# A decoder trunk whose order is planned: other planner costs, and three tables that move single operations

## The chip, the cores and the metric

The kernel runs on one core of a Trainium2 chip. The core has a matrix engine (TensorE, PE in the profile; its weight loads are PEld), a vector engine (VectorE, DVE), a scalar engine (ScalarE, ACT), a general engine (GpSimd, POOL) and an engine that issues most of the DMAs (SyncE, SP). Every engine runs its own queue in order; they wait for each other through semaphores. The metric is device time in microseconds (us) of one execution, lower is better. Three runs of the kernel before the change took 999.25, 1002.59 and 1001.85 us: a median of 1001.85 us.

## The reference

Two decoder layers work on 256 tokens of width 1024, all in FP32. Each layer adds to `x`, in this order: half a SwiGLU feed-forward (width 2816), a mixer, another half feed-forward, and a gated per-layer embedding. Every one of these reads an RMS norm of `x` and its result is normed again before it is added. The mixer of layer 0 is an mLSTM with 4 heads (two chunks of 128 tokens, exponential gates, a running state); that of layer 1 is differential attention with 8 head pairs, which reads keys and values that were computed once, after layer 0.

```python
for layer in range(DEPTH):
    g = norm_g[layer]
    h = swiglu(rms_norm(x, g[0]), w_ffn_in[layer, 0], w_ffn_out[layer, 0])
    x = x + 0.5 * rms_norm(h, g[1])
    h = rms_norm(x, g[2])
    # layer 0: mlstm_mixer(h, ...), layer 1: diff_attention(h, k_sh, v_sh, ...)
    x = x + rms_norm(h, g[3])
    h = swiglu(rms_norm(x, g[4]), w_ffn_in[layer, 1], w_ffn_out[layer, 1])
    x = x + 0.5 * rms_norm(h, g[5])
    gate = jax.nn.sigmoid(rms_norm(x, g[6]) @ w_ple_gate[layer])
    e = p[layer].astype(x.dtype) @ w_ple_proj[layer]
    x = x + rms_norm(e * gate, g[7])
    if layer == N_A_LAYERS - 1:
        k_sh, v_sh = shared_kv(x, kv_norm, w_kv)
```

## The kernel before

**The work.** The 256 tokens are two row tiles of 128 (`t` is 0 or 1). A weight comes from memory in pieces of 128 x 2048 FP32 (tag `wraw`, ten buffers), is copied by ScalarE into a rounded part (`whi`, six buffers), and VectorE subtracts this from the original to get the remainder (`wlo`, five buffers). Activations are split in the same way (`xh`/`xl`, and `hh`/`hl` for the hidden layer of a feed-forward). A product is then three fast matmuls, high by high, high by low and low by high (`mm3`, line 569). Blocks of a feed-forward's input matrix go mostly in pairs, in a scheme with seven products instead of eight (`block_pair`, line 780); it needs sums of weight blocks, some of which VectorE makes and some an accumulating DMA that GpSimd issues. `forms` (line 762) makes the matching sums of activations. Attention, gates and the mLSTM's inner products use plain FP32 matmuls, which the profile shows as two instructions each.

**Between the blocks** stands a norm: ScalarE squares and sums two halves (`squares`), GpSimd adds the two sums and takes the power -0.5 (`rnorm`, line 632), VectorE adds the scaled result to `x` (`add_to_x`), TensorE transposes `x` (`transpose4`), and the transposed pieces are scaled and split (`gained`, line 710).

**The mLSTM** (line 1072) computes queries, keys and gates, then the values as a block pair, then for each head an exponential and a product (`head`, line 1157), then the outputs of both row tiles (`outputs`, line 1191) with an output gate (another block pair) and an output projection. **Differential attention** is at line 1282.

**The order.** The body is not issued as it is written. `Notes` records every operation with what it must come after; consecutive plain FP32 matmuls or transposes into the same tile count as one operation, and an operation's number is its place in this list (6290 in all). `cost` (line 215) gives each a duration and a latency. `play` (line 309) then simulates the five engines: TensorE takes the ready operation of lowest rank (its place in the program), with a penalty `PEN` where the kind of matmul changes; SyncE takes its loads by rank; ScalarE, VectorE and GpSimd take the ready operation that is due first. Due times come from `backward` (line 270), which counts back from the end of the schedule played before. Ten rounds are played, the best one's due times are used, and all instructions are issued in the resulting order from one line, 495, so that the profile knows them by tile names. An edge between two operations is stored as `after[earlier] = True` (the later one needs the earlier one's result) or `False` (it only has to start after it).

**The start.** ScalarE issues the load of `x0` (the first 128 columns of the transposed input, with gains) and that of another piece of the transposed input (line 596); eight matmuls on a zeroed tile (line 612) run until the first data is there.

## Time and profile before

| | us |
|---|---|
| median of three runs | 1001.85 |
| the profiled execution | 999.12 |
| its span, first to last instruction | 997.3 |
| TensorE busy | 979.6 |
| VectorE busy | 897.7 |
| ScalarE busy | 714.6 |
| GpSimd busy | 95.1 |

A row of the profile's timeline shows the start, the duration, the engine, line, operation, the tile written and those read, the shapes, how often, and in brackets how long the engine stood idle before it and what ended that. Rows of the stretches give, for each window of time, busy microseconds of each engine with the number of instructions, then the granted share of TensorE's clock, the busy share of the DMA engines, and GB/s. Ends of matmuls are modelled, so starts are the better measure. Where the stages lie in the span: feed-forward 1 of layer 0 to about 200 us, mLSTM to about 298, feed-forward 2 to about 480, embedding and keys to about 530, feed-forward 1 of layer 1 to about 695, differential attention to about 797, feed-forward 2 to about 965, then the last embedding.

### The profile page before, as it was taken

To read this page: it belongs to the slowest core of one execution; us is meant where nothing else is said; L and a number is where in the kernel's file an instruction comes from. 1 tells how busy PE (TensorE), PEld (TensorE's weight loads), DVE (VectorE), ACT (ScalarE), POOL (GpSimd) and SP (SyncE) were. 2 spreads that over 40 slices of the span, in tenths; PEclk is the share of its full clock that TensorE was granted. 3 is DMA by queue.
4 is the path that set the end of the run, shared out by engine and by line. 5 is a ranking of instruction groups with operands and counts; after the bars stand their busy time and mean duration, and the time that the engine had idled before them with its cause. 6 is when DMAs were issued, how large, how long until landed. Compare 5 with 4: busy or idle time off the path is not lost. (4 is left out here: it accounts for less than half of the span.)

```text
span 997.3 us, 12405 instructions
## 1 busy us (share of the span) xinstructions
PE 979.6 (98%) x4594; PEld 799.1 (80%) x4594; DVE 897.7 (90%) x898; ACT 714.6 (72%) x954; POOL 95.1 (10%) x133
## 2 busy tenths in 40 slices
PE   8999999999999999999999999999999999999997
PEld 7878888887777788888878888887888877888886
DVE  6999999789989999998798999898875899999983
ACT  7678667588857776776877867687766778767763
POOL 0000000300231000001120000001102200000010
PEclk9999999999999999999999999999999999999999
DMA  9999956976899999766799999764758899996721
GB/s 344 417 312 342 288 217 240 286 246 197 310 346 303 334 295 291 295 244 223 265 312 323 341 346 348 307 253 153 253 211 256 252 284 348 298 281 242 285 85 43
DMA packets 45861, 274.70 MB, mean 275 GB/s; under 512 B 5480, under 2 KB 5864, under 8 KB 16104
## 3 DMA queue, kind: packets, MB, share of 16 engines
q1 hardware_dynamic: 39752, 231.69, 60.8%
q0 software_dynamic: 5760, 41.95, 20.6%
q8 instruction: 36, 0.59, 0.2%
q10 hardware_dynamic: 288, 0.27, 0.1%
q14 instruction: 25, 0.20, 0.1%
HBM read 263.40 MB, written 10.49 MB: 275 GB/s over the span
## 5 line engine op out<-in xcount | busy, mean ns | idle before, releaser
L495 DVE TENSOR_TENSOR wraw<-wraw,wraw 128x2048 f32<-128x2048 f32 x44 | 100.7, 2288 | 0.2
L495 ACT ACTIVATE whi_0r<-wraw 128x2048 fp32r<-128x2048 f32 (+2 forms) x51 | 82.0, 1610 | 10.6 <-PE accI L495 5.7
L495 ACT ACTIVATE whi_2r<-wraw 128x2048 fp32r<-128x2048 f32 (+1 forms) x49 | 79.4, 1633 | 7.5 <-DMA wraw<-in_ffn_in 3.5
L495 ACT ACTIVATE whi_4r<-wraw 128x2048 fp32r<-128x2048 f32 (+1 forms) x45 | 75.3, 1683 | 11.3 <-PE accI L495 5.2
L495 ACT ACTIVATE whi_3r<-wraw 128x2048 fp32r<-128x2048 f32 (+1 forms) x47 | 77.6, 1657 | 8.0 <-PE accI L495 2.5
L495 ACT ACTIVATE whi_1r<-wraw 128x2048 fp32r<-128x2048 f32 (+2 forms) x50 | 74.4, 1502 | 11.6 <-PE accI L495 9.2
L495 ACT ACTIVATE whi_5r<-wraw 128x2048 fp32r<-128x2048 f32 (+1 forms) x43 | 71.8, 1675 | 11.3 <-DVE wraw L495 4.8
L495 ACT ACTIVATE att<-accI 128x512 f32<-128x512 f32 x84 | 49.7, 593 | 39.9 <-PE accI L495 38.7
L495 POOL DMA_DIRECT2D wraw<-in_ffn_in x36 | 32.0, 890 | 336.3 <-DMA wraw<-in_ffn_in 250.4
L495 POOL TENSOR_SCALAR sm<-sm 128x1 f32<-128x1 f32 x32 | 20.7, 648 | 296.6 <-ACT sg L495 295.2
L495 ACT ACTIVATE sg<-att,sm 128x256 f32<-128x256 f32 x57 | 28.3, 504 | 22.7 <-DVE att L495 21.5
L495 POOL TENSOR_TENSOR sm<-sm,mhalf 128x1 f32<-128x1 f32 (+2 forms) x40 | 33.1, 828 | 105.1 <-DVE sm L495 102.6
L495 ACT ACTIVATE sg<-accO 128x512 bf16<-128x512 f32 (+2 forms) x46 | 20.3, 446 | 23.5 <-PE accO L495 17.5
L495 DVE SCALAR_TENSOR_TENSOR wraw<-wraw,sm,wraw 128x512 f32<-128x512 f32 x32 | 22.7, 750 | 13.0 <-POOL sm L495 13.0
L495 PEld LDWEIGHTS tr<-ident,sg 128*128 128x128 f32 x176 | 23.3, 140 | 13.7 <-DVE hl_2r L495 1.9
L495 PE MATMUL tr<-ident,sg 128*128 128x128 f32 x176 | 34.0, 274 | 0.0
L495 DVE TENSOR_TENSOR att<-accI,att 128x512 f32<-128x512 f32 x42 | 28.5, 686 | 2.6 <-PE accI L495 2.6
L495 ACT ACTIVATE sg<-wraw 128x512 bf16<-128x512 f32 x32 | 20.0, 626 | 13.7 <-DVE wraw L495 9.5
L495 DVE SCALAR_TENSOR_TENSOR sg<-att,sm,sg 128x256 f32<-128x256 f32 x57 | 26.5, 483 | 2.0 <-ACT sg L495 2.0
L495 ACT ACTIVATE att<-accI,sm 128x512 f32<-128x512 f32 (+1 forms) x22 | 14.7, 669 | 17.3 <-PE accI L495 17.3
L495 ACT ACTIVATE hh_1r<-tr 128x256 fp32r<-128x256 f32 x30 | 11.3, 378 | 20.1 <-PE accO L495 12.8
L495 DVE TENSOR_TENSOR att<-att,att 128x512 f32<-128x512 f32 (+1 forms) x35 | 23.5, 672 | 1.0 <-ACT att L495 0.9
(612 smaller groups left out, 3251.8 us busy)
## 6 DMA issues: line engine op xcount, KB each, us to landing
wraw<-in_ffn_in SPq DMA_DIRECT2D x102, 1024.0 KB, 7.7
wraw<-in_ffn_out SPq DMA_DIRECT2D x44, 1024.0 KB, 9.2
wraw<-in_ffn_in POOLq DMA_DIRECT2D x36, 1024.0 KB, 13.4
wraw<-in_mlstm_in SPq DMA_DIRECT2D x14, 1024.0 KB, 6.4
wraw<-in_ple_gate SPq DMA_DIRECT2D x8, 1024.0 KB, 5.0
wraw<-in_w_kv SPq DMA_DIRECT2D x8, 1024.0 KB, 4.8
home<-wraw SPq DMA_DIRECT2D x28, 256.0 KB, 5.3
wraw<-home SPq DMA_DIRECT2D x14, 512.0 KB, 4.6
```

Source lines behind the costliest of these rows:

```text
L495: getattr(getattr(self.nc, eng), name)(*args, **kw)
```

## The change

The operations stay the same but for two. What is new:

- Durations: a plain FP32 matmul on 128 rows now costs at least 222 ns where it was at least 105, one on 64 rows 124; a ScalarE operation with a sum costs 60 ns more; only a change between 64-row matmuls and others costs TensorE time in the plan (150 ns), all other changes of kind 5 ns, and the ordering penalty follows the same rule.
- ScalarE's two loads must keep their program order.
- Ten warm-up matmuls instead of eight.
- After the rounds, three tables are applied and the plan is played once more: `FIRST` adds edges (the second operation may only start after the first has started), `SHIFT` adds nanoseconds to due times, and `MOVE` adds to the rank of one or several operations in a row.

```diff
@@ -26,6 +26,44 @@
 ROUNDS = 10
+FIRST = (
+    (4319, 4321), (4319, 4385), (5365, 5244), (5365, 5188), (2092, 2061), (5251, 5220), (5057, 5062), (5222, 5423),
+    (5201, 5235), (4318, 4325), (1595, 1441), (1505, 1440), (1440, 1455), (1535, 1499), (5140, 5139), (4977, 5020),
+    (4975, 5025), (2063, 2264), (2208, 2044), (1464, 1470), (1480, 1500), (1482, 1476), (1664, 1538), (1538, 1458),
+    (1550, 1536), (1480, 1454), (1544, 1547),
+)
+SHIFT = (
+    (138, -12166828), (147, 7213), (173, 7287), (175, 10522), (205, -28563), (266, -41996), (269, -35620),
+    (295, -84784), (331, -55484), (334, -54491), (337, -88941), (338, -45024), (340, -31781), (341, -161489),
+    (343, -108617), (344, -203509), (346, -52943), (386, -11814), (390, -53670), (393, -34537), (394, -168189),
+    (396, -162608), (1308, -58533), (1309, -97295), (1310, -103560), (1313, -111190), (1314, -170957), (1317, 44789),
...
+    (1349, 37223), (1356, -59146), (1359, 29562), (1386, 10525), (1439, -4376737), (1440, -2725461), (1441, -454410),
+    (1454, -4503563), (1455, -3045380), (1458, -4439452), (1460, -152237), (1461, -270420), (1462, -36478),
+    (1464, -4378085), (1466, -175520), (1467, -318667), (1468, -28162), (1470, -4525640), (1472, -2771036),
+    (1473, -2239202), (1474, -44584), (1476, -9725501), (1478, -6966893), (1479, -8294119), (1480, -3303077),
+    (1482, -7409750), (1499, -5487120), (1500, -3890822), (1501, -13100380), (1503, -1333004), (1505, -1059340),
+    (1508, -1816243), (1536, -7027061), (1538, -3542943), (1540, -3727262), (1542, -3900808), (1544, -2367321),
+    (1547, -3499927), (1548, -6014694), (1549, -5635368), (1550, -5657865), (1978, -5999), (1983, -11331),
+    (2043, -7859), (2072, -3500), (2085, -2500), (4197, 1808), (4216, -3878), (4973, -34218), (4977, -25713),
...
+    (5231, -16772), (5244, -26804), (5251, -15422),
+)
+MOVE = (
+    (140, 1, -9250), (183, 1, -1100), (184, 1, -1800), (186, 1, 200), (211, 1, -3350), (212, 1, -2000), (223, 1, 300),
+    (224, 1, 400), (1392, 3, -900), (1395, 1, -700), (1396, 2, -600), (1398, 1, -400), (1442, 1, -11350),
+    (1443, 1, -11600), (1444, 1, -11550), (1445, 1, -11100), (1446, 1, -8250), (1447, 1, -9500), (1448, 1, -7800),
+    (1456, 1, -10550), (1459, 1, -850), (1465, 1, -800), (1471, 1, -2650), (1475, 1, -500), (1477, 1, -700),
+    (1481, 1, -11400), (1510, 1, -950), (1511, 1, -10900), (1512, 1, -10650), (1513, 1, -10350), (1514, 1, -3950),
+    (1559, 1, -4000), (1564, 1, -4550), (1566, 1, -4400), (1568, 1, -4500), (1871, 1, 200), (1877, 1, 300),
+    (4287, 1, -50), (4294, 1, -50), (4296, 1, -50), (4298, 1, -50), (4300, 1, -50), (4342, 1, 400), (4351, 1, 300),
+    (4420, 5, -250), (4970, 1, -200), (4974, 1, -200), (5030, 1, -450), (5032, 1, -750), (5088, 1, -150),
...
+    (5204, 1, -2800), (5221, 1, -2350), (5226, 1, -3250),
+)
...
+        if o.name == "dma_start" and eng == "scalar":
+            if self.ringed is not None:
+                o.after[self.ringed] = False
+            self.ringed = o
...
-        return ins[0].ap[0][1], ins[0].ap[-1][1]
+        return "h" if ins[0].ap[0][1] == 64 else "f"
...
-                o.dur = max(n * 4 / 2.4 / (2 if ins[0].ap[0][1] == 64 else 1) + 6, 70 if n * 4 < P else 105)
-                if n == 1:
-                    o.dur = 210
+                o.dur = 124 if ins[0].ap[0][1] == 64 else max(n / 0.6 + 6, 222)
...
-            o.dur = 0.83 * m + (100 if sb_in else 72) + (90 if ptr else 0) + (90 if sums else 0)
+            o.dur = 0.83 * m + (100 if sb_in else 72) + (90 if ptr else 0) + (150 if sums else 0)
...
-        return 0 if o.kind == before or {o.kind, before} == {"r", "t"} else PEN
+        return PEN if (o.kind == "h") != (before == "h") else 0
...
-                        end += 10 if {o.kind, before} == {"r", "t"} else 110
+                        end += 150 if "h" in (o.kind, before) else 5
...
-    for i in range(8):
+    for i in range(10):
         nc.tensor.matmul(warm[:, :P], wz, wz, start=True, stop=True)
...
-    plan.play(MARGIN, due[ends.index(min(ends))])
+    due = due[ends.index(min(ends))]
+    plan.play(MARGIN, due)
+    for before, then in FIRST:
+        plan.ops[then].after.setdefault(plan.ops[before], False)
+    for i, ns in SHIFT:
+        due[plan.ops[i]] += ns
+    for i, n, by in MOVE:
+        for o in plan.ops[i:i + n]:
+            o.rank += by
+    plan.play(MARGIN, due)
```

## The prediction

> **What bounds the kernel now.** I read the page's span and engine lines first, then TensorE's waits, then busy time by stretch, and last the timeline around each wait.

> ```profile
> span 997.3 us, 12405 instructions
> PE 979.6 (98%) x4594; PEld 799.1 (80%) x4594; DVE 897.7 (90%) x898; ACT 714.6 (72%) x954; POOL 95.1 (10%) x133
> ```

> TensorE is busy for 979.6 of 997.3 us, and the change takes no matrix work away. An order of the same operations can only win back the 17.7 us in which TensorE stands still, and the little that each restart costs. The profiled execution took 999.12 us, 1.8 us more than its span. The three runs shown are 999.25, 1001.85 and 1002.59 us, so this execution stands at their low end, 2.7 us under their median.

> TensorE's waits (us in total, times, longest):

> ```profile
> PE accI L495 <- DVE wraw L495: 1.5, 1, 1.5
> PE accO L495 <- DVE wraw L495: 1.5, 1, 1.5
> PE accI L495 <- DVE xh_0r L495: 1.5, 1, 1.5
> PE accO L495 <- ACT whi_3r L495: 1.4, 1, 1.4
> PE accI L495 <- ACT att L495: 1.3, 3, 0.7
> PE tr L495 <- DVE wraw L495: 0.4, 2, 0.2
> PE accI L495 <- DVE xl_6r L495: 0.5, 1, 0.5
> ```

> Single waits in many places, none that repeats through the run. Busy time by stretch (us, then PE, PEld, DVE, ACT, POOL busy) says what stands beside them:

> ```profile
> 25.00:175.00 150.00, 148.62 (x671) 121.04 (x670) 147.26 (x120) 108.38 (x107) 6.71 (x12) 1.00 0.88 303
> 215.00:268.00 53.00, 50.40 (x225) 39.74 (x224) 50.14 (x67) 48.41 (x77) 4.80 (x3) 1.00 0.79 259
> 268.00:290.00 22.00, 22.00 (x105) 18.06 (x104) 19.55 (x25) 10.86 (x19) 5.39 (x6) 1.00 0.95 279
> 290.00:350.00 60.00, 57.79 (x258) 46.17 (x258) 58.00 (x49) 45.27 (x51) 8.74 (x9) 1.00 1.01 336
> 690.00:704.00 14.00, 13.28 (x69) 10.67 (x68) 10.94 (x15) 10.13 (x19) 5.82 (x8) 1.00 0.35 105
> 790.00:850.00 60.00, 59.46 (x268) 47.49 (x267) 58.75 (x54) 47.35 (x51) 7.43 (x9) 1.00 0.95 309
> 850.00:950.00 100.00, 100.00 (x455) 81.60 (x453) 98.24 (x81) 71.44 (x74) 1.72 (x2) 1.00 0.79 268
> 950.00:1000.00 50.00, 40.24 (x208) 33.97 (x207) 27.28 (x38) 20.75 (x43) 6.95 (x13) 0.95 0.18 64
> ```

> TensorE's idle time is length less PE: 1.38 us in the first feed-forward block (25 to 175), 2.60 in the mLSTM's values, heads and gates (215 to 268), 2.21 where the second block starts, 0.72 where diff-attention starts, 0.54 where the last block starts. Of the 9.8 us in the last row, 2.7 lie behind the span's end and the rest is the final norm and store, which no table touches. VectorE has 2.74 us idle in 25 to 175 and 1.25 in 790 to 850: there it is a second bound.

> **What a stall costs.** Around 60 us:

> ```profile
> 58.23 0.40 PE L495 MATMUL accI<-wlo_2r,xh_4r 128*128 128x512 f32 x1
> 58.01 1.91 ACT L495 ACTIVATE whi_3r<-wraw 128x2048 fp32r<-128x2048 f32 x1 [0.41 <-ACT att L495]
> 59.98 0.51 PE L495 MATMUL accO<-whi_3r,hh_1r 128*128 128x512 f32 x1 [1.35 <-ACT whi_3r L495]
> 60.33 0.39 PE L495 MATMUL accI<-wlo_3r,xh_6r 128*128 128x512 f32 x1
> 60.56 0.40 PE L495 MATMUL accI<-whi_1r,xl_6r 128*128 128x512 f32 x1
> ```

> Undisturbed matmuls start 0.23 us apart (60.33 to 60.56). Across the stall it is 1.75 and then 0.35, so 1.52 + 0.12 = 1.64 us are lost where 1.35 show as idle: a toll of 0.28 us per stall, which I add below.

> **The change part by part.** Numbers in the tables count the noted operations; I followed each to its instruction in the trace.

> *The two loads on ScalarE's queue* now keep program order, x0 first:

> ```profile
> 0.72 0.41 ACTq L495 DMA_DIRECT2D wraw<-in_xT  x1
> 1.16 0.45 ACTq L495 DMA_DIRECT2D att<-in_x  x1
> 1.04 3.58 PE L495 MATMUL tr<-sg 128*128 128x128 f32 x16 [1.04 <-DVE sg L495]
> 5.64 0.29 DVE L495 TENSOR_SCALAR xh_0r<-att 128x128 fp32r<-128x128 f32 x1 [4.65 <-DMA att<-in_x]
> 6.07 0.47 PE L495 MATMUL accI<-whi_0r,xh_0r 128*128 128x512 f32 x1 [1.45 <-DVE xh_0r L495]
> ```

> x0 ends the first real wait, and is issued 1.16 - 0.72 = 0.44 us sooner. Between 0 (the next loads are no earlier) and 0.44 I take **-0.3**, since TensorE then runs almost without a hole up to 20 us.

> *Two more warm-up matmuls* are four instructions of 3.58/16 = 0.22 us, 0.9 us behind the end at 4.62. The hole up to 6.07 (5.6 with x0 sooner) covers them: **0**. Without that cover they would cost 0.9.

> *First feed-forward block.* The entries from 138 to 396 let the Silu at 19.45 and its transposes run as soon as they can, and make fourteen conversions and adds of weights or sums due 12 to 204 us sooner, so that VectorE takes them whenever they are ready. They aim at 0.21 us idle at 20.5 and 1.35 at 60. Bounds 0 and 1.64; with VectorE at 147.26 of 150 I take half, **-0.8**: what TensorE gains at 60, VectorE must deliver sooner at 75 to 175.

> *mLSTM.* Entries 1308 to 1568 give some eighty operations an order of their own: the heads' exponentials and products, the value copies, the splits between them (due up to 13 ms sooner, so at once when ready) and the matmuls of outputs(0) (rank about 4500 lower, ahead of everything).

> ```profile
> 222.81 0.50 PE L495 MATMUL accI<-whi_2r,xh_3r 128*128 128x512 f32 x1 [0.33 <-ACT att L495]
> 257.63 0.50 PE L495 MATMUL accI<-whi_3r,xh_4r 128*128 128x512 f32 x1 [0.69 <-ACT att L495]
> 265.89 0.47 PE L495 MATMUL accO<-whi_1r,xh_0r 128*128 128x512 f32 x1 [1.45 <-DVE wraw L495]
> ```

> Full gain: 2.60 idle and three tolls, 3.44 us; none: 0. ScalarE is at 48.41 of 53 here but has 11 us free from 268 to 290, so some of its work can wait. What is late next is the weight split 1500, which FIRST now puts behind the last head's exponential, and the block pair's matmuls on it. Two thirds: **-2.3**.

> *Start of the second block* (1978 to 2264):

> ```profile
> 293.19 3.14 POOL L495 TENSOR_SCALAR sm<-sm 128x1 f32<-128x1 f32 x1 [7.43 <-ACT sg L495]
> 293.95 2.29 DVE L495 TENSOR_TENSOR wraw<-wraw,wraw 128x2048 f32<-128x2048 f32 x1
> 297.81 0.66 PE L495 MATMUL accI<-ident,wraw 128*128 128x128 f32 x4 [1.48 <-DVE wraw L495]
> ```

> 1.48 of its 2.21 us hangs on GpSimd's 3.14 us sum, which no entry names. Of the other 0.73 and three tolls (1.6) I take **-0.3**.

> *Start of diff-attention.* FIRST puts 4318 (the split xh_6r) ahead of a square and 4319 (xl_6r) ahead of 4321 (the second att product):

> ```profile
> 693.61 0.61 ACT L495 ACTIVATE sg<-wraw 128x512 bf16<-128x512 f32 x1
> 693.64 0.69 DVE L495 TENSOR_TENSOR att<-accI,gcol 128x512 f32<-128x512 f32 x1
> 694.22 0.61 ACT L495 ACTIVATE xh_6r<-att 128x512 fp32r<-128x512 f32 x1
> 695.42 0.68 DVE L495 TENSOR_TENSOR xl_6r<-att,xh_6r 128x512 fp32r<-128x512 f32 x1
> 696.15 0.50 PE L495 MATMUL accI<-whi_1r,xl_6r 128*128 128x512 f32 x1 [0.47 <-DVE xl_6r L495]
> ```

> xh_6r can start 0.6 us sooner and xl_6r about 1, more than the wait of 0.47: 0.75 with its toll, out of 1.28 for both stalls here. **-0.85**.

> *Start of the last block* (4970 to 5423): 5201, the add that frees an accumulator, goes ahead of the 2.29 us add 5235, which then waits some 3 us, and with it the two splits of its weight. The stretch holds 0.54 us and three tolls, 1.4; VectorE is full up to 950 (98.24 of 100), so **-0.6**, bounds 0 and 1.4.

> *Corrected durations* cost no instruction, but re-sort VectorE, ScalarE and DMAs everywhere, also where no table repairs it. Each conversion that moves also moves the release of its raw buffer, and with it SyncE's next load and everything behind that in the queue. The trace cannot show the new order. From above it is at most the stalls already counted; from below, the second rival. I take **+0.6**.

> Sum: -0.3 - 0.8 - 2.3 - 0.3 - 0.85 - 0.6 + 0.6 = **-4.55 us**. From 999.12 that is 994.6, from the median of 1001.85 it is 997.3. Rows don't say why the runs differ; I take the middle, **996.0**.

> **Rivals.**
> *VectorE takes the gain back.* In 25 to 175 and 790 to 950 it is at 98%, so each stall removed returns as a wait for a split, and the mLSTM's as a wait for the split that was put back. Only x0 and diff-attention stay, about 1.2: 997.9 and 1000.7, the middle 999.3. Against it: ScalarE's free time after 268. It is also where the tables would end if they no longer fit the order they shift.

> *GpSimd is blocked at the layer ends* (the slower side). Its sums and powers behind each norm:

> ```profile
> L495 POOL TENSOR_TENSOR sm<-sm,mhalf x40: 559/568/2455, 18.7 to 992.3; 128x1 f32<-128x1 f32 x32, 128x4 f32<-128x4 f32 x4, 128x2 f32<-128x2 f32 x4
> L495 POOL TENSOR_SCALAR sm<-sm x32: 292/302/3138, 18.3 to 989.0; 128x1 f32<-128x1 f32 x32
> ```

> Minimum, median, maximum in ns: 302 normally, 3138 at 293, ending as the 2.29 us VectorE add beside it ends. A re-sorted VectorE can put such an add beside any norm. Price 1.48 + 0.28 = 1.76 us of TensorE for each that matters; it decides once the matmuls left cover less than the 2.84 us of delay. Three more against a gain of 1.2 make +4.1: 1003.2 and 1005.9, the middle 1004.6. For it: one of these is already on the path. Against: TensorE's only other waits on a norm (tr for wraw, above) come to 0.4 us.
> [...]

> *The start decides the spread.* If the 2.6 us between the median and the lowest run arise in the first microseconds and the longer warm-up removes them, the median falls to 999.25 - 4.55 = 994.7. For it: the hole of 1.45 us after the warm-up. Against: the granted clock shows no start in the page's slices.
> [...]

> *Everything comes off:* 0.44 + 1.64 + 3.44 + 1.6 + 1.28 + 1.4 = 9.8 us, 989.3 and 992.1: 990.7.

> **How the numbers follow.** Forecast 0.53 (its own range 992 to 999), VectorE 0.22, GpSimd 0.13, start 0.08, everything 0.04; 0.3% (3 us) is about what this kernel's measurement can tell. Faster: most of 0.53, and 0.12: 0.60. Same: VectorE's 0.22 and a little of the first: 0.27. Slower: 0.13. Range 991 to 1002: it takes in VectorE's case at either base and leaves out the whole of GpSimd's and part of the last.

> **What would show it.** Right: TensorE idle falls from 2.60 us to under 1 in the mLSTM stretch; no wait for xl_6r near 695; the first real matmul near 5.6; the whi_3r wait near 60 gone or halved. VectorE's rival: the same waits, 10 to 100 us further on, for wlo or whi tiles. GpSimd's: a sum or power of over 2 us just ahead of transposes that wait for wraw. The forecast is wrong if TensorE's idle time stays above 16 us, or drops below 9.

## The result, and the profile after

The changed kernel takes **990.85 us** (median of four runs, 990.61 to 991.39). The kernel before, timed beside it, takes 1001.14 us. The ratio is 0.9899, with a 95% interval of 0.988 to 0.9918: 1.0% faster. I had forecast 996.0 with a range of 991 to 1002. The direction is right; the time lies 0.15 us below the lower end, and the gain is about twice the forecast one.

The two profiled executions took 999.12 us before and 990.61 us after: 8.5 us, which is also the difference of the spans. The medians differ by 10.3 us, since the profiled execution of before was one of its quickest. Over all comparisons below, before had medians of 1000.2 to 1000.44 us, so its usual time is some 9.5 us above the new kernel's.

The page's span and busy time of the engines, after (to be read against the first fence of the prediction):

```profile
span 988.8 us, 12411 instructions
PE 977.0 (99%) x4598; PEld 798.9 (81%) x4598; DVE 896.0 (91%) x898; ACT 714.7 (72%) x954; POOL 99.7 (10%) x133
```

TensorE now stands still for 988.8 - 977.0 = 11.8 us instead of 17.7. That explains 5.9 of the 8.5 us. The other 2.6 us left TensorE's *busy* time, although it has four more instructions. The prediction did not count on anything of the kind beyond the toll of 0.28 us per stall.

TensorE's waits after (us in total, times, longest):

```profile
PE tr L536 <- DVE wraw L536: 1.1, 1, 1.1
PE tr L536 <- DVE sg L536: 1.0, 1, 1.0
PE accI L536 <- ACT att L536: 0.7, 1, 0.7
PE accI L536 <- DVE wlo_1r L536: 0.7, 1, 0.7
PE accI L536 <- ACT whi_1r L536: 0.5, 1, 0.5
PE accI L536 <- DVE wlo_0r L536: 0.2, 1, 0.2
```

Six waits of over 0.15 us are left; the second is the one ahead of the warm-up. The waits for `whi_3r`, `xh_0r` and `xl_6r` are gone. Of the 11.8 us of idle time, 7.1 lie behind the last matmul, after as before; ahead of it 10.6 us have become 4.7.

The same stretches as in the prediction, after (us, then PE, PEld, DVE, ACT, POOL busy, granted clock, DMA share, GB/s):

```profile
25.00:175.00 150.00, 150.00 (x676) 122.01 (x676) 147.82 (x122) 108.92 (x107) 7.50 (x13) 1.00 0.88 307
215.00:268.00 53.00, 51.06 (x229) 39.79 (x228) 50.10 (x65) 46.96 (x77) 4.00 (x4) 1.00 0.76 252
290.00:350.00 60.00, 58.88 (x269) 47.64 (x267) 59.14 (x52) 46.60 (x52) 9.22 (x8) 1.00 0.97 321
690.00:704.00 14.00, 14.00 (x79) 11.20 (x79) 12.66 (x16) 9.17 (x23) 4.70 (x6) 1.00 0.64 228
790.00:850.00 60.00, 60.00 (x269) 48.45 (x269) 59.73 (x54) 46.38 (x52) 7.95 (x6) 1.00 1.00 330
```

The first feed-forward, the start of diff-attention and the start of the last block have no idle time left (1.38, 0.72 and 0.54 before). The mLSTM keeps 53 - 51.06 = 1.94 of its 2.60 us, and the start of the second block 1.12 of 2.21. All of this is idle time. What a stage really gained is seen when both executions are set side by side at points where TensorE has done the same work, and the times are compared. Matmuls are matched by count and size, so these differences are good to some 0.1 us:

| TensorE's work, by its time before | after less before, us | predicted |
|---|---|---|
| up to 22 us (start) | -0.60 | -0.3, and part of -0.8 |
| 57 to 109 (first feed-forward) | -1.30 | rest of -0.8 |
| 200 to 281 (mLSTM) | -0.37 | -2.3 |
| 291 to 303 and 313 to 420 (second block) | -0.84 and -1.2 | -0.3 |
| 420 to 692 | -0.1 | 0 |
| 692 to 704 (start of diff-attention) | -1.03 | -0.85 |
| 704 to 787 (rest of diff-attention) | -1.8 | 0 |
| 818 to 850 (last block) | -1.21 + 0.33 | -0.6 |
| the rest | -0.4 | +0.6, over the whole run |
| sum | -8.5 | -4.55 |

Three rows do not fit: the mLSTM gave a sixth of what I expected, the second block several times as much, and diff-attention behind its start 1.8 us for which I had no term at all.

Two rows of the table, the start's and the mLSTM's, are partly chance of this one execution, as the runs below show. The matmul that starts at 20.48 us before and at 19.87 here starts between 20.38 and 21.15 in e3, e4, e6, e7 and e8, which all load x0 first. And the wait for `whi_1r` at 224 us stands in none of e4, e5, e7 and e8, which have the same mLSTM; there the mLSTM row is -1.2. The two all but cancel in the sum: e4's span is 989.0 us.

### The profile page after: what moved, and what is told of

Read it like the earlier page. It is cut to its first block, busy times and chain, and to the rows that moved or that the text cites. A ratio compares the mean times of both kernels' runs of the same rounds, so it can differ in the third digit from the quotient of the medians.

```text
span 988.8 us, 12411 instructions
## 1 busy us (share of the span) xinstructions
PE 977.0 (99%) x4598; PEld 798.9 (81%) x4598; DVE 896.0 (91%) x898; ACT 714.7 (72%) x954; POOL 99.7 (10%) x133
## 5 line engine op out<-in xcount | busy, mean ns | idle before, releaser
L536 ACT ACTIVATE whi_0r<-wraw 128x2048 fp32r<-128x2048 f32 (+2 forms) x49 | 79.5, 1633 | 12.7 <-DVE wraw L536 4.7
L536 ACT ACTIVATE whi_1r<-wraw 128x2048 fp32r<-128x2048 f32 (+2 forms) x50 | 77.7, 1567 | 8.4 <-DVE wraw L536 4.0
L536 ACT ACTIVATE whi_3r<-wraw 128x2048 fp32r<-128x2048 f32 (+1 forms) x46 | 74.2, 1616 | 10.4 <-PE accI L536 4.4
L536 ACT ACTIVATE whi_5r<-wraw 128x2048 fp32r<-128x2048 f32 (+1 forms) x46 | 77.3, 1688 | 5.9 <-PE accI L536 3.3
L536 POOL TENSOR_SCALAR sm<-sm 128x1 f32<-128x1 f32 x32 | 29.1, 909 | 287.2 <-ACT sg L536 281.7
L536 ACT ACTIVATE sg<-att,sm 128x256 f32<-128x256 f32 x57 | 28.4, 502 | 18.7 <-DVE att L536 17.9
L536 POOL TENSOR_TENSOR sm<-sm,mhalf 128x1 f32<-128x1 f32 (+2 forms) x40 | 28.9, 722 | 101.5 <-DVE sm L536 98.9
L536 DVE TENSOR_TENSOR wlo_0r<-wraw,whi_1r 128x2048 fp32r<-128x2048 f32 (+1 forms) x13 | 25.3, 1955 | 3.8 <-PE accI L536 3.5
L536 ACT ACTIVATE hh_2r<-tr 128x256 fp32r<-128x256 f32 x30 | 11.3, 378 | 21.2 <-PE tr L536 10.1
L536 DVE TENSOR_TENSOR wlo_2r<-wraw,whi_0r 128x2048 fp32r<-128x2048 f32 (+1 forms) x12 | 25.2, 2108 | 1.4 <-ACT whi_0r L536 1.1
```

Of the source, the lines that this page charges most:

```text
L536: getattr(getattr(self.nc, eng), name)(*args, **kw)
```

## The experiments

The 12 kernels below were timed in three groups, each beside runs of the kernel before. Ratios are to these runs, with their 95% interval.

### Costs, tables and start, each alone

*e1: the corrected durations and the new start, with empty tables.*

```diff
-FIRST = (
-    (4319, 4321), (4319, 4385), ...
+FIRST = ()
-SHIFT = (
-    (138, -12166828), (147, 7213), ...
+SHIFT = ()
-MOVE = (
-    (140, 1, -9250), (183, 1, -1100), ...
+MOVE = ()
```

> The changed kernel with the three tables emptied: corrected durations, x0 loaded first and ten warm-up matmuls stay. Theory T (the tables hold the gain): only the start's 0.6 to 0.7 us comes off, the time stays within 2 us of before (about 1000.5), and the 64-row matmuls of diff-attention still stand in five runs. Theory C (the corrected durations hold a good part): the 64-row matmuls fall into four runs, diff-attention gets about 1.7 us shorter, and the time is 998 or lower.

Measured: 997.25 us (996.54 to 1003.85, 12 runs), ratio 0.9981 [0.9968, 0.9994], span 995.3. With the new start the re-sort wins about 3 us of median and 2.0 us of span (the ratio says 1.9, because two of the 12 runs lie above 1001), where I had put +0.6 for it alone. But it makes one stall longer, as e1's timeline shows:

```profile
694.86 0.68 DVE L504 TENSOR_TENSOR xl_6r<-att,xh_6r 128x512 fp32r<-128x512 f32 x1
695.60 0.50 PE L504 MATMUL accI<-whi_1r,xl_6r 128*128 128x512 f32 x1 [1.50 <-DVE xl_6r L504]
```

The wait for `xl_6r` is 1.50 us; before it was 0.47. The whole is faster in spite of it, mostly between 704 and 790 us (-1.6) and 291 and 303 us (-1.26).

*e2: the tables and the new start, on the old durations and the old rule for a change of kind.*

```diff
-        return "h" if ins[0].ap[0][1] == 64 else "f"
+        return ins[0].ap[0][1], ins[0].ap[-1][1]
...
-                o.dur = 124 if ins[0].ap[0][1] == 64 else max(n / 0.6 + 6, 222)
+                o.dur = max(n * 4 / 2.4 / (2 if ins[0].ap[0][1] == 64 else 1) + 6, 70 if n * 4 < P else 105)
+                if n == 1:
+                    o.dur = 210
...
-            o.dur = 0.83 * m + (100 if sb_in else 72) + (90 if ptr else 0) + (150 if sums else 0)
+            o.dur = 0.83 * m + (100 if sb_in else 72) + (90 if ptr else 0) + (90 if sums else 0)
...
-        return PEN if (o.kind == "h") != (before == "h") else 0
+        return 0 if o.kind == before or {o.kind, before} == {"r", "t"} else PEN
...
-                        end += 150 if "h" in (o.kind, before) else 5
+                        end += 10 if {o.kind, before} == {"r", "t"} else 110
```

> The changed kernel with the durations and the penalty for a change of matmul kind put back to those of before; tables, load order and warm-up stay. Theory A (the tables are corrections of single stalls that hold by themselves): most of the gain stays, under 994 us. Theory B (they only fit the order that the corrected durations give): the gain is gone, 999 us or more, with new waits of 1 to 2 us for wlo or whi tiles where entries move operations past each other.

Measured: 1001.35 us (1000.33 to 1003.15, 10 runs), ratio 1.0012 [1.0003, 1.0021], span 998.7. TensorE's longest waits in e2:

```profile
PE accO L538 <- DVE att L538: 2.1, 1, 2.1
PE accI L538 <- ACT whi_3r L538: 1.8, 1, 1.8
PE accI L538 <- ACT att L538: 1.5, 2, 0.7
```

On the other durations, the same entries make new and longer waits in the mLSTM: 2.1 us at 244.3 and 1.8 us for a `whi_3r` at 248.6. Behind the first of them the granted clock drops, and stands at 0.50 from 246 to 252 us:

```profile
245.00:253.00 8.00, 6.20 (x17) 3.95 (x16) 8.00 (x8) 7.38 (x17) 0.00 (x0) 0.57 0.79 285
```

6.20 us of matmuls at a mean clock of 0.57 lose some 2.7 us, an estimate from this row. All ten runs of e2 have a mean clock of 0.994 to 0.996, where e3's have 0.996 to 0.999, so the drop is probably in all of them. With e3 below, these are the four corners, all but the last measured with the same runs of before:

| | without tables | with tables |
|---|---|---|
| old durations, new start | 999.81 (e3) | 1001.35 (e2) |
| new durations, new start | 997.25 (e1) | 990.85 (the change) |

The tables win 6.4 us on the new durations and lose 1.5 us on the old ones. The loss has one place. Set beside e3 by equal work, e2 is 4.4 us longer in the mLSTM (200 to 281 us), the clock included, and 0.9 longer at 303 to 420; it is 2.6 us shorter at 290 to 303, 1.1 at 692 to 704 and 0.7 at 810 to 850. So, by place, the mLSTM's entries are repairs to one particular order and do harm on another. The later ones win on either, though not the same amounts.

*e3: only the new start, on the kernel before.*

```diff
+        if o.name == "dma_start" and eng == "scalar":
+            if self.ringed is not None:
+                o.after[self.ringed] = False
+            self.ringed = o
...
-    for i in range(8):
+    for i in range(10):
```

> The kernel before with only its start changed: x0 loaded first and ten warm-up matmuls. Ledger: the first real matmul comes 0.6 to 0.75 us sooner and all else stays, so -0.6 us, and the runs spread as widely as those of before (3 us). Theory S (the start makes the spread of before): the median falls by 2 us or more, to the lowest runs of before, and the runs agree within 1 us.

Measured: 999.81 us (999.01 to 1001.31, 11 runs), ratio 0.9996 [0.9987, 1.0004], span 997.9. The timeline of its first microseconds:

```profile
4.75 0.50 PE L506 MATMUL accI<-whi_0r,xh_0r 128*128 128x512 f32 x1
...
5.89 0.50 PE L506 MATMUL accI<-wlo_0r,xh_0r 128*128 128x512 f32 x1 [0.40 <-DVE wlo_0r L506]
...
7.35 0.51 PE L506 MATMUL accI<-whi_0r,xh_0r 128*128 128x512 f32 x1 [0.27 <-ACT whi_0r L506]
...
8.08 0.51 PE L506 MATMUL accI<-wlo_0r,xh_0r 128*128 128x512 f32 x1 [0.22 <-DVE wlo_0r L506]
```

The first real matmul starts at 4.75 instead of 6.07, without any wait. But now it waits for the copies and remainders of the first weights, and by 22 us only 0.08 us of the 1.3 is left. The load of x0 ended last, with these close behind.

*e4: the change with eight warm-up matmuls.*

```diff
-    for i in range(10):
+    for i in range(8):
```

> The changed kernel with eight warm-up matmuls instead of ten. Theory S: some runs are 1.5 to 3 us longer than the changed kernel's 990.6 to 991.4, with a lower granted clock at the start. Otherwise: the same time within 0.5 us and the same spread.

Measured: 990.89 us (990.77 to 990.97, 4 runs), ratio 0.9906 [0.9891, 0.992], span 989.0. The two warm-up matmuls make no difference, neither to the median nor to the spread.

### The tables, a part at a time

Each of these takes all entries of one range of operation numbers out of the three tables and leaves the rest of the change.

```diff
 e5: -  (138, -12166828), ... (396, -162608)  in SHIFT, (140, 1, -9250) ... (224, 1, 400) in MOVE
 e6: -  12 pairs of FIRST, 54 entries of SHIFT and 27 of MOVE with numbers from 1000 to 1600
 e7: -  15 pairs of FIRST, 26 entries of SHIFT and 36 of MOVE with numbers above 1600
```

*e5: without the entries of the first feed-forward (numbers below 1000).*

> The changed kernel without the table entries of the first feed-forward block (operations below 1000). If its gain stands on its own: the wait of some 1.4 us for a split weight near 57 to 60 us comes back and the rest of the trace stays, 992 to 992.5 us. If VectorE gives it back further on (the prediction's first rival): within 0.4 us of the changed kernel.

Measured: 993.74 us (992.88 to 996.12, 4 runs), ratio 0.9938 [0.9919, 0.9957], span 991.1. Its profile loses 2.3 us against the changed kernel: about 1 by 21 us and 1.2 between 57 and 107 us. The first of these is not shown to be the entries' work, since e4, e6 and e7, which have them, lose 0.7 to 1.3 us there as well. At the second this wait stands, in a stage where the changed kernel has none:

```profile
59.97 0.51 PE L674 MATMUL accI<-wlo_3r,xh_6r 128*128 128x512 f32 x1 [0.88 <-DVE wlo_3r L674]
```

Of this loss at most 0.3 us comes back by 200 us. So VectorE, 98% busy in this stage, does not take the gain back.

*e6: without the mLSTM's entries (numbers 1000 to 1600, more than half of SHIFT).*

> The changed kernel without the table entries of the mLSTM (operations 1000 to 1600). The prediction's step: they are worth 2.3 us, so 993.2. By the ledger of the two profiled runs, in which the stretch 200 to 280 us gained 0.4 us and the kernel without tables gained the same there: nothing, 990.9 within 0.5 us, with other waits in that stretch but the same sum.

Measured: 990.27 us (990.12 to 990.79, 4 runs), ratio 0.9899 [0.9883, 0.9916], span 989.0. For the whole kernel these entries are worth nothing. The mLSTM's stretch and its largest waits in e6:

```profile
215.00:268.00 53.00, 50.42 (x228) 40.06 (x228) 50.50 (x66) 47.72 (x76) 4.78 (x3) 1.00 0.77 258
```

```profile
256.05 2.00 PE L611 MATMUL accO<-wraw,att 128*128 128x257 f32 x8 [0.76 <-DVE wraw L611]
264.11 0.47 PE L611 MATMUL accO<-whi_3r,xh_0r 128*128 128x512 f32 x1 [0.70 <-DVE wraw L611]
```

And the changed kernel's, with the entries:

```profile
244.52 0.50 PE L536 MATMUL accI<-wlo_1r,xh_1r 128*128 128x512 f32 x1 [0.72 <-DVE wlo_1r L536]
250.86 0.50 PE L536 MATMUL accI<-whi_0r,xh_5r 128*128 128x512 f32 x1 [0.75 <-ACT att L536]
```

2.58 us idle without, 1.94 with, and the same time. The entries remove the waits for the heads' products at 256 and 264 and put waits for a weight's remainder and for a head's `att` at 244.5 and 250.9 in their place. In the comparison by equal work of the changed kernel with the one before, the same is seen: -1.68 us between 259 and 270, where the wait of 1.45 was, and +1.9 between 224 and 247. Of the latter 0.7 hang on a wait that is not the entries' doing. It stands in the changed kernel's profile alone; e4, e7 and e8 run the same matmuls in the same order there (e5 too, with other buffers) and lack it. The wait, and e4's stretch without it:

```profile
224.09 0.50 PE L536 MATMUL accI<-whi_1r,xh_0r 128*128 128x512 f32 x1 [0.46 <-ACT whi_1r L536]
```

```profile
215.00:268.00 53.00, 51.52 (x231) 40.52 (x230) 50.76 (x66) 47.59 (x77) 4.17 (x4) 1.00 0.77 256
```

So with the entries the mLSTM has about 1.5 us of idle time and is 1.2 us shorter than before from 200 to 281 us; in e6, without them, it is 0.4 to 0.5 us shorter. The entries do win some 0.7 us in their own stage, and lose it at the norm behind it. From 291 to 303 us e6 is 0.7 us shorter than the changed kernel and 1.1 shorter than e4: TensorE's wait near 296 is 0.43 us in e6, 1.12 and 1.51 in those two, behind a GpSimd sum that is as long in all three (4.29, 4.21, 4.21).

*e7: without the entries above 1600 (second block, diff-attention, last block).*

> The changed kernel without the table entries from operation 1600 on (second feed-forward block, diff-attention, last block). By the ledger against the kernel without tables: 1.4 us at 300 to 420, 2.3 us at 692 to 704 (the wait for xl_6r comes back), 1.2 us at 818 to 829, so 4.9 us and 995.8. The prediction's steps for the same places say 0.3 + 0.85 + 0.6 = 1.75 us, so 992.6.

Measured: 996.1 us (995.49 to 998.63, 7 runs), ratio 0.9958 [0.9943, 0.9972]. Its profiled execution was its slowest (998.63, span 996.9), so I use its places and not its sum. Against the changed kernel it loses 2.4 us at 288 to 300, 1.4 at 310 to 345, 2.3 at 688 to 698 and 1.2 at 810 to 841, the three starts that the entries name. Most of the first is not the entries' worth but the clock, which drops to a half behind a wait of 2.06 us:

```profile
297.58 0.66 PE L627 MATMUL tr<-ident,wraw 128*128 128x128 f32 x4 [2.06 <-DVE wraw L627]
```

```profile
298.00:302.00 4.00, 4.00 (x17) 3.29 (x15) 3.42 (x7) 3.43 (x9) 1.78 (x3) 0.57 0.90 179
```

4.00 us of matmuls at a mean clock of 0.57 lose 1.7 us, an estimate from this row. The loss at 697 is e1's wait again:

```profile
697.20 0.50 PE L627 MATMUL accI<-whi_3r,xl_6r 128*128 128x512 f32 x1 [1.50 <-DVE xl_6r L627]
```

So what the tables win lies in the entries that e5 and e7 leave out: 2.9 and 5.3 us by medians (together more than the tables' 6.4, so they overlap). The mLSTM's add nothing to the whole.

### GpSimd at the start of the second block

The prediction's slower rival rests on GpSimd's sums being blocked by VectorE's adds. In the changed kernel this happens at the same place as before, and worse. From its timeline:

```profile
290.18 2.28 DVE L536 TENSOR_TENSOR wraw<-wraw,wraw 128x2048 f32<-128x2048 f32 x1
290.55 4.21 POOL L536 TENSOR_SCALAR sm<-sm 128x1 f32<-128x1 f32 x1 [7.14 <-ACT sg L536]
292.38 2.29 DVE L536 TENSOR_TENSOR wlo_3r<-wraw,whi_4r 128x2048 fp32r<-128x2048 f32 x1
295.43 1.41 DVE L536 SCALAR_TENSOR_TENSOR wraw<-wraw,sm,wraw 128x512 f32<-128x512 f32 x2 [0.76 <-POOL sm L536]
296.24 0.66 PE L536 MATMUL tr<-ident,wraw 128*128 128x128 f32 x4 [1.12 <-DVE wraw L536]
```

The sum takes 4.21 us: it starts during one add and ends with the *second*. *e8* puts the second one, and two like it, behind the norm:

```diff
 FIRST = (
+    (1809, 1888), (1809, 1866), (4968, 5048),
```

> The changed kernel with three more pairs in FIRST: VectorE's second add of the norm's result to x (1809) ahead of the splits 1888 and 1866, and 4968 ahead of the add 5048. So VectorE waits for GpSimd instead of starting another operation with two SBUF inputs. If GpSimd is blocked for as long as such operations follow each other: the sum near 290.5 takes under 2.4 us instead of 4.21, the transposes of x lose their wait of 1.12 us near 296, and that place gets 1.4 us shorter. If the sum is slow for another reason it stays above 4 us. The moved splits may cost the same again: 989.5 to 991.5 in all.

Measured: 992.07 us (992.01 to 992.93, 4 runs), ratio 0.992 [0.9905, 0.9934], span 990.3. The place itself, in e8's timeline:

```profile
289.85 2.28 DVE L537 TENSOR_TENSOR wraw<-wraw,wraw 128x2048 f32<-128x2048 f32 x1
290.21 2.08 POOL L537 TENSOR_SCALAR sm<-sm 128x1 f32<-128x1 f32 x1 [7.17 <-ACT sg L537]
...
293.78 0.66 PE L537 MATMUL tr<-ident,wraw 128*128 128x128 f32 x4 [0.62 <-DVE wraw L537]
294.31 2.29 DVE L537 TENSOR_TENSOR wlo_3r<-wraw,whi_4r 128x2048 fp32r<-128x2048 f32 x1
```

The mechanism is confirmed: with one add in the way the sum ends with that one, after 2.08 us, and TensorE's wait falls from 1.12 to 0.62. The whole kernel is still slower than the changed one, by 1.2 us. The repair wins 0.43 us here and loses 0.49 at 310 to 325, 0.65 at 446 and 1.04 at 800, where other tiles (`xl_3r`, `hl_2r`, an `att`) are now late. The loss at 446 may be chance, for e5 has one of 0.5 us there without the pairs. The three pairs were not tried apart.

### The rule for changes of kind

In diff-attention the scores (`accO<-wraw,wraw`) are matmuls on 64 rows, for the two heads of a pair on rows 0 to 63 and 64 to 127 in turn; between their groups stand matmuls on 128 rows. Before, the plan charged 110 ns and an ordering penalty for most changes of kind; the change charges only a change into or out of 64 rows. *e9* puts this rule alone into the kernel before, without new durations, tables or start.

```diff
-        return ins[0].ap[0][1], ins[0].ap[-1][1]
+        return "h" if ins[0].ap[0][1] == 64 else "f"
...
-        return 0 if o.kind == before or {o.kind, before} == {"r", "t"} else PEN
+        return PEN if (o.kind == "h") != (before == "h") else 0
...
-                        end += 10 if {o.kind, before} == {"r", "t"} else 110
+                        end += 150 if "h" in (o.kind, before) else 5
```

> The kernel before with one part of the corrected durations alone: a change of matmul kind costs 150 ns in the plan where 64-row matmuls begin or end and 5 ns elsewhere, and the ordering penalty follows; no other duration, no table. If this rule is what shortens diff-attention: the 64-row matmuls stand in four runs instead of five, and 704 to 790 us gets 1.6 to 1.7 us shorter. If the corrected FP32 durations do it: five runs, and no gain there. The other stretches move by 1 to 2 us either way, so the whole time says little.

Measured: 993.2 us (992.01 to 993.58, 4 runs), ratio 0.9921 [0.9907, 0.9935], span 991.8. Alone, these three lines give 7.2 us by medians, where the whole change gives some 9.5. What they do in diff-attention is seen in the timeline of before, round its last scores:

```profile
729.73 0.40 PE L495 MATMUL accI<-whi_3r,xl_2r 128*128 128x512 f32 x1
730.05 2.05 PE L495 MATMUL accO<-wraw,wraw 64*128 64x128 f32 x24
732.03 0.39 PE L495 MATMUL accO<-hl_1r,hh_1r 128*128 128x256 f32 x1
732.35 1.16 PE L495 MATMUL accO<-wraw,wraw 64*128 64x128 f32 x8
733.44 0.50 PE L495 MATMUL accI<-whi_0r,xh_0r 128*128 128x512 f32 x1
```

and of the changed kernel:

```profile
724.12 0.39 PE L536 MATMUL accI<-whi_0r,xl_2r 128*128 128x512 f32 x1
724.43 2.16 PE L536 MATMUL accO<-wraw,wraw 64*128 64x128 f32 x32
726.52 0.50 PE L536 MATMUL accI<-whi_5r,xh_0r 128*128 128x512 f32 x1
```

Before, one 256-wide matmul splits the 32 instructions into 24 and 8, and from the matmul ahead to the matmul behind it takes 733.44 - 729.73 = 3.71 us; unsplit it takes 2.40. The matmul in between must run somewhere, at an estimated 0.12 us (half of the 0.23 between two undisturbed 512-wide ones); the other 1.2 us are the split. TensorE shows no idle time in either, so no wait tells of it. The scores stand in four groups (16, 32, 16, 32) in e1, e9 and the changed kernel alike, against five before, and from 704 to 790 us these three gain 1.6, 1.5 and 1.8 us. So the split is most of it, and the rest, 0.3 to 0.6 us, was not traced.

The rest of e9's 5.5 us of span comes from elsewhere: -2.19 at 291 to 303, where the wait of 1.48 behind GpSimd is gone, -1.12 at 692 to 704 and -0.76 at 57 to 109. The rule also moves matmuls there (it no longer charges a change between fast and plain 128-row matmuls); which of them matter was not tried.

*e10: e1 with the three pairs of FIRST that name xl_6r's split.*

```diff
-FIRST = ()
+FIRST = ((4319, 4321), (4319, 4385), (4318, 4325))
```

> The kernel without tables, and with three pairs of FIRST alone: 4318 ahead of 4325, 4319 ahead of 4321 and of 4385. Without them TensorE waits 1.5 us for xl_6r near 695 us. If single stalls are worth their idle time and a toll of 0.28 us: that wait goes, the stretch of 690 to 704 us gets 1.5 to 2.3 us shorter and the whole 1.5 to 2.3 us less than the 997.25 of the kernel without tables: 995 to 995.7. If VectorE gives it back, the wait reappears within 20 us and the time stays at 997.

Measured: 997.07 us (996.49 to 997.65, 5 runs), ratio 0.9963 [0.995, 0.9976], span 994.9. The wait for `xl_6r` is gone, and 692 to 704 is 2.40 us shorter than in e1. But the plan behind it comes out otherwise, and in e10 the scores stand in six groups:

```profile
702.72 1.16 PE L505 MATMUL accO<-wraw,wraw 64*128 64x128 f32 x16
...
710.94 1.26 PE L505 MATMUL accO<-wraw,wraw 64*128 64x128 f32 x16
...
712.56 1.26 PE L505 MATMUL accO<-wraw,wraw 64*128 64x128 f32 x16
...
720.37 1.16 PE L505 MATMUL accO<-wraw,wraw 64*128 64x128 f32 x16
...
727.75 2.05 PE L505 MATMUL accO<-wraw,wraw 64*128 64x128 f32 x24
...
730.04 1.16 PE L505 MATMUL accO<-wraw,wraw 64*128 64x128 f32 x8
```

The stages with a split group lose 0.47 and 1.14 us, and with smaller losses elsewhere 0.4 us of span is left of the 2.4. One edge repairs one stall and re-sorts everything behind it.

### Can the plan do better?

*e11 and e12* add more pairs to FIRST, chosen only because the plan's own end falls: in e11 131 pairs on top of e6 (planned end 983.5 to 982.5 us), in e12 two pairs that keep GpSimd free at 290 us and 154 others (982.6).

```diff
 e11: FIRST = (the pairs left in e6) + 131 more
 e12: FIRST = (the pairs left in e6) + ((1809, 1888), (1809, 1866)) + 154 more
```

> The changed kernel without the table entries of the mLSTM, and with 131 more pairs of FIRST that shorten the planner's own schedule by 1.0 us (983.5 to 982.5). If the planner's end still tells the chip's time to some tenths: 989.3. If what is left are waits that the planner doesn't know (GpSimd beside VectorE, loads at the start): 990.3, as without these pairs.

> As the kernel before in this list (no mLSTM entries, more pairs: 154, planner's end 982.6), and VectorE's add 1809 ahead of the splits 1888 and 1866, so that GpSimd's sum behind the mLSTM isn't blocked for two VectorE operations. If that wait (0.4 to 1.1 us near 296) is real and nothing gives it back: 988.7 to 989.5, the fastest of all. If the moved splits cost it again, as they did with the changed kernel: 990 to 990.5.

Measured: e11 992.59 us (991.57 to 993.32, 5 runs), ratio 0.9915 [0.9903, 0.9928]; e12 991.01 us (990.49 to 991.54, 4 runs), ratio 0.9901 [0.9888, 0.9915]. Neither beats e6, from which both start. The plan ends 5.9 us ahead of the measured span in the changed kernel (982.9 and 988.8) and 8.2 us in the kernel before (989.1 and 997.3): a microsecond in the plan is below what it knows of the chip.

No kernel here is clearly faster than the changed one: e6's 990.27 us and e12's 991.01 us cannot be told from its 990.85 us.

## Why the prediction was right and wrong, step by step

- **x0 first, -0.3: too large.** e3 measured -0.08 by 22 us. Its bound of 0 ("the next loads are no earlier") is what happened. The -0.60 of the changed kernel's own execution is luck, as said below the table. The first real matmul, forecast near 5.6, starts at 5.33 in the changed kernel and at 4.75 in e3, with the same start: the 20 warm-up instructions took 4.60 us in the one and 3.91 in the other.
- **Two warm-up matmuls, 0: right** (e4). The hole covers them.
- **First feed-forward, -0.8: mis-sized.** The wait at 60 is gone whole, not halved: -1.30 from 57 to 109, and e5 gives 1.2 there. I took half because VectorE is 98% busy; its 2.74 us of idle time in 25 to 175 were enough (2.18 are left).
- **mLSTM, -2.3: wrong.** It gave -0.37, or -1.2 without the chance wait at 224, and e6 shows that its entries give the whole kernel nothing. The failed step is "two thirds" of a bound that assumed each wait gone without a successor. The old wait at 266 did go (-1.68), but a weight's remainder became late at 244 and an `att` at 251 (0.72 and 0.75), the kind of successor that I had named and priced at a third. The 0.7 us that the entries still win here are lost at the norm behind the mLSTM, which I counted as another stage. My sign for it, under 1 us of idle time in this stretch, failed too: 1.94, and 1.5 in e4.
- **Start of the second block, -0.3: too small.** It gave -0.84 and -1.2, and e7 without its entries loses 3.8 us there, 1.7 of them by the clock. I assumed that a wait behind GpSimd which no entry names would stay. It did: 1.12 for 1.48 here, 1.51 in e4, and GpSimd's sum even took longer, 4.21 for 3.14. The rest of the stage, to 420 us, gained as much again, and there I had no term.
- **Start of diff-attention, -0.85: right.** -1.03. Of the step as written, the wait goes, and xl_6r comes sooner by 0.6 us (3.87 us behind the start of the add to `x`, against 4.47). But xh_6r comes only 0.06 sooner, since ScalarE now waits for its `att`. In the changed kernel's timeline:

```profile
689.62 0.63 ACT L536 ACTIVATE xh_6r<-att 128x512 fp32r<-128x512 f32 x1 [0.45 <-DVE att L536]
690.28 0.69 DVE L536 TENSOR_TENSOR xl_6r<-att,xh_6r 128x512 fp32r<-128x512 f32 x1
```

- **Start of the last block, -0.6: about right**, -0.9.
- **Corrected durations, +0.6: wrong in sign, and the main error.** I bounded their gain "at most the stalls already counted". That is false: they change how long TensorE is *busy*. The rule for changes of kind keeps the groups of 64-row matmuls whole, some 1.2 of the 1.5 to 1.8 us in diff-attention, and no wait shows it. e1 gives about -3 us for all costs and the start, e9 -7.2 us for the rule alone; so the rest of e1 costs some 4 us on top of the rule, and the tables then win 6.4. I read the diff's line on the changes of kind as a planner's detail and did not look for 64-row matmuls in the trace.
- **The tables are tied to their durations.** I treated the entries as additive. The four corners say -6.4 us on one set of durations and +1.5 on the other, where the mLSTM alone loses 4.4.

The rivals: **VectorE takes the gain back** falls with e5, except in the mLSTM, where one of the two new waits (`wlo_1r` at 244) is of its kind. **GpSimd blocked** has a true mechanism (e8: 2.08 us instead of 4.21 with the second operation moved away), and the blocked sums did spread: three of over 2 us before, seven after. But the path hardly felt it: TensorE waits for over 0.15 us behind two of them before (1.48 and 0.17 us) and behind one after (1.12). **The start decides the spread** falls: with the new start on the old order (e3) the runs still scatter over 2.3 us, with the new order and the old warm-up (e4) over 0.2. A clock at a half did cost e7's profiled execution an estimated 1.7 us, but at 298 us and not at the start. **Everything comes off** has nearly the right time (8.5 of its 9.8 us, between the two profiled executions), but not by its way: TensorE keeps 11.8 us of idle time, within the 9 to 16 that I had set for the forecast, and most of the mLSTM's; 2.6 of the 8.5 us are busy time.

What stays open: which matmuls the rule for changes of kind moves at 57, 291 and 692 us, and most of the spread of the runs. It is under 1 us in the changed kernel, e4, e6 and e8, 1 to 2 in e9 to e12, and 2 to 7 in before, e1, e2, e3, e5 and e7 (of which most have more runs). It comes with the order and not with the start. The clock has a part in it. Of the 29 runs of before in the first group, the 14 with a mean granted clock of 0.998 or more have a median of 999.7 us, the 15 below it 1000.9. A clock that drops behind a long wait in some executions, as in e7's, would do this; it is shown in that one execution of e7 and in e2's, and argued for the rest.

## What to carry to other kernels

Idle time bounds what re-ordering can win only if the order does not change what the busy time costs: look for instructions that run side by side (here the pairs of 64-row matmuls, where one split cost 1.2 us), and compare start to start across each group, before taking "length less busy" as the most there is. A table of single shifts is tied to the costs under which it was made; measure all four corners of costs and tables before crediting either, and look by stage at where they differ. Before a stage is priced from one trace, set a second execution of the same order beside it and read the granted clock there: here a chance wait cost 0.7 us, and a drop of the clock 1.7. And where a wait is removed in a stage whose other engines are nearly full, count it only once you have found that nothing else there ends within the same microsecond.

## What the runs showed of the hardware

**A blocked GpSimd stayed blocked across back-to-back VectorE operations.** The sum with a median of 0.30 us took 4.21 us in the changed kernel, over `wraw<-wraw,wraw` and `wlo_3r<-wraw,whi_4r` (2.28 and 2.29 us), and 2.08 us in e8, over the first of these alone. It did not get in between the two. The 3.14 us of the kernel before, which the prediction puts down to one add of 2.29 us, are of the same kind: a remainder of 1.22 us runs right ahead of that add, at 293.95.

```profile
292.82 1.22 DVE L495 TENSOR_TENSOR wlo_0r<-wraw,whi_1r 128x1024 fp32r<-128x1024 f32 x1
```

**The granted clock halved behind two waits of 2 us.** It stood at 0.50 for 3.4 us behind the wait of 2.06 us in e7, and in e2 for 6.8 us, from 1.2 us after the end of the wait of 2.09 us on, with that of 1.80 inside; TensorE then started 512-wide matmuls 0.42 to 0.59 us apart instead of 0.23. Behind 1.95 us (e3, at 298.6) and 2.24 us (e11, at 296.7) it stayed at 1.00. The mean clocks of the four executions agree: 0.997 in e7 and 0.995 in e2, 0.998 in e3 and e11, as in before and after. What decides between the two was not found.

**An earlier first load moved nothing.** The first matmul started 1.3 us sooner in e3, and 0.08 us of it was left 16 us later.
